# RWKV-7 and short-convolution block on one core: the off-diagonal 16x16 corners of the 32x32 inverses computed on VectorE instead of TensorE, and the last chunk's Gram blocks issued with the others

## The chip, the cores and the metric

The kernel runs on one core of one Trainium2 chip. The metric is the device time of one launch in microseconds; the time before is the median of three runs. Beside those, one execution was profiled.

## The reference, cut to what matters

A block takes 512 tokens of width 2048, prepends 16 meta tokens, normalises them and multiplies by one input projection of 65 column tiles of 128. Half of the columns feed a short gated convolution, the other half an RWKV-7 recurrence over 16 heads of 64. Both results go through an output projection, a residual and a last norm.

```
P = rmsnorm(h) @ w_in                      # r, k, v, g, lora | B, C, h, gc
S_t = S_{t-1} diag(w_t) - (S_{t-1} kk_t)(kk_t*a_t)^T + v_t k_t^T
y_t = S_t r_t
y_a = (groupnorm(y) + bonus) * silu(g);   y_b = B * conv3(C*h) * silu(gc)
out = rmsnorm(h + concat(y_a, y_b) @ w_out)[meta:]
```

The recurrence is run in nine chunks of 64 steps (the meta tokens are padded to the first). In chunk form every head and chunk needs the inverse of a 64x64 unit-like triangular matrix built from the Gram products of its keys. That inverse is what the change is about.

## The kernel before

The input projection is one long stream of matmuls, the generator `mains` (line 483). Its tiles follow `plan` (line 102): k, r and v of a pair of heads, g, and then C, h, B and gc of the convolution. One tile is 16 steps of three matmuls (high and low parts of weights and activations), for k, v, r, g, C and h in two column halves, so 96 matmuls and two PSUM banks; B and gc have 48 of 512 columns and one bank. The banks come from the pool `pm`, which has four. The tile's result is evacuated by `use` (line 400), mostly on VectorE (`scaled`, line 346). Weights are loaded by `prefetch` (line 138) into three raw buffers and split by `split_w` into six quarter slots: ScalarE casts the high part (line 134), VectorE or GpSimd subtracts the low part (line 135). The column offset of a quarter in its slot comes from `column` (line 115).

All else is placed in this stream by hand. TensorE's order is the program's order. `fill(ns)` (line 551) advances the stream by so many ns of projection, counted as 0.43 ns a column, and `later(ns, fn)` (line 532) traces a DMA when the clock of the stream has come so far; such DMAs are queued on SyncE behind the last weight load that was traced. The other engines' orders are chosen by a scheduler from priorities and expected times; `ahead()` raises a priority, and `issue_after` puts instructions behind a given one on its engine, without waiting for its result.

For each pair of heads i, `prepare(i)` (line 627) makes the operands, then the Gram blocks (`gram`, line 679): nine chunks and two heads, 18 matmuls of 64x128, eight chunks in one group and chunk 8 in a second group after `fill(FW["gram2"])`, together with the key norms `n2` and the bonus sums `zb`. `masked` (line 688) takes them to SBUF as `gt` on VectorE. The triangles go to DRAM (`sg`), and their 16x16 diagonal blocks come back as `d`, one block per partition, 72 partitions. VectorE inverts them there by doubling (lines 769 to 789) into `y`. The blocks of `y` go to DRAM into `sx` (`blocks`, line 737), from which `load_inverse` (line 793) reads 64x64 matrices `xT` and, at swapped partitions, `xo`.

After every two pairs, `invert` (line 831) joins the blocks in two levels on TensorE. Level one makes the 16x16 corners of the 32x32 inverses: transposes `xn` on VectorE (line 844), a group of 64 matmuls (line 853), a copy to SBUF on ScalarE (line 860), a second group of 64 (lines 867 and 869), and then on VectorE a copy under the mask `ms` (line 877), transposes `xm` (line 880) and a copy of half of it to `xo` (line 884). Level two does the same with 32x32 blocks (lines 893 to 918). The result is stored to DRAM for the recurrence (`recur`, line 940), which follows the last `invert` and is again woven into the stream. Then `split_mix` and the output projection finish the kernel.

Of the kernel before, what the change touches and what calls it, by code (L numbers as in the profile page):

```python
# [18 lines left out]
P = 128  # L19
# [5 lines left out]
CH = 64  # L25
# [16 lines left out]

FW = dict(
    evac=34, start=1062, lora=2200, gram=8000, gram_b=13500, gram2=5500, misc=2000, v=2000, vt=1000, solve=24500, solve_first=30000,
    tr=3200, lev=3000, cp=4200, out=1500, begin=19500, p=2900, u=2900, s=5200, last=3700, mix=2600,
)


# [29 lines left out]
def hymba_kernel(ctx: ExitStack, tc: tile.TileContext, xt, xtok, front, w_in, w_out, pv, lup, cst, msk, gf, out):  # L78
# [84 lines left out]
    ms = cq.tile([P, CH], I32, name="ms")  # L163
    ident = cs[:, C_ID : C_ID + P]
    gmask = cs[:, C_GM : C_GM + 256].rearrange("p (h c) -> p h c", h=2)
    pm = ph1.enter_context(tc.tile_pool(name="pm", bufs=4, space=PSUM))
# [119 lines left out]
        for kt in range(KT - 5, KT):  # L286
            square_x(kt)
    nc.sync.dma_start(cs, cst)
    nc.sync.dma_start(ms, msk)
    zt = tm("zt")  # L290
    nc.gpsimd.memset(zt, 0.0)
    for b in range(2):
# [43 lines left out]
    def main(j, ranges, name):  # L336
        prefetch(2 * j + 4)
        ps = banks(ranges, name, pm, "main")
        for k4 in range(4):
            if k4 == 1:  # L340
# [56 lines left out]
    def behind_of(what):  # L397
        return tc.issue_after(state.pop(what)) if what in state else nullcontext()

    def use(what, i, ps):  # L400
        if what == "lora":
            use_lora(ps)
        elif what in ("k", "v"):
            t = cq.tile([P, LP], F32, tag=what, name=f"{what}{i}")
            nc.gpsimd.memset(t[:, META:CH], 0.0)
            shift_full(ps, tile_of[what] + i, f"{what}{i}", padded(t))
            got[what, i] = t
        elif what in ("r", "g"):
            t = cq.tile([P, SEQ], F32, tag=f"r{i % 2}" if what == "r" else "g", name=f"{what}{i}")
            shift_real(ps, tile_of[what] + i, f"{what}{i}", t)  # L410
            if what == "g":
                gate(t, f"r{i}")
                later(14000, lambda: nc.sync.dma_start(gated[i], t))
            got[what, i] = t
        elif what == "C":
            u = tm(f"u{i}")
            scaled(TAIL, ps, u, 14)
            got[what, i] = u
        elif what == "h":
            u = got["C", i]  # L420
            hh = tm(f"hh{i}")
            with behind_of("turned"):
                scaled(TAIL, ps, hh, 14)
            n = SEQ + 2
            nc.gpsimd.tensor_tensor(out=u[:, 0:n], in0=u[:, 0:n], in1=hh[:, 0:n], op=ALU.mult)
            cv = tp.tile([P, SEQ], F32, tag="cw", name=f"cv{i}")
            nc.scalar.activation(cv, u[:, 0:SEQ], AF.Copy, scale=col(V_CW, i))
            for j in (1, 2):
                nc.vector.scalar_tensor_tensor(
                    out=cv, in0=u[:, j : j + SEQ], scalar=col(V_CW, 8 * j + i), in1=cv, op0=ALU.mult, op1=ALU.add  # L430
                )
            got[what, i] = cv
# [21 lines left out]
    ready = set()  # L454
    direct = {}

    def token_scale_sums():
# [74 lines left out]
    def later(ns, fn):  # L532
        pending.append((clock[0] + ns, fn))
        pending.sort(key=lambda e: e[0])
# [92 lines left out]
    def prepare(i):  # L627
# [82 lines left out]
        zn = pi.tile([2, 288], F32, tag="misc", name=f"n2_{i}")  # L710
        zs = ((zn, 0, 288), (ze[0][0:2, P : P + 288], 288, LP))
        for z, a, b in zs:
            nc.tensor.matmul(z, ones[:, P : P + 2], sqh[:, a:b], start=True, stop=False)
            nc.tensor.matmul(z, ones[:, P : P + 2], sql[:, a:b], start=False, stop=True)
# [3 lines left out]
        with ahead():  # L718
            for z, a, b in zs:
                nc.scalar.copy(n2[0:2, a:b], z)  # L720
            masked([z[:, 0:P].unsqueeze(1) for z in ze], 8, 9)
        nc.scalar.copy(r, zb)
        fill(FW["misc"])

# [76 lines left out]
                    ),  # L801
                )

        later((22500 if i == 1 else 20500) if p else 29000, lambda: nc.sync.dma_start(blocks(sx), y))
        later((24500 if i == 1 else 22500) if p else 33000, load_inverse)

        for h, hs, ho in heads:
            for b in range(2):
# [17 lines left out]
                    64 * (1 - b // 2) + 32 * t, 32,  # L826
                )
        fill(FW["vt"])
        return dict(gt=gt, xT=xT, xo=xo, i=i)

    def invert(two):
        first = two[0]["i"]
        both = range(2)
        fill(FW["solve"] + 2400 * (first == 2) if first else FW["solve_first"] + 1100)
        run_pending(float("inf"))


        def wide(name):
            return tr(name)[:, 0 : 8 * CH].rearrange("p (q k s) -> p q k s", q=2, s=CH)
# [2 lines left out]
        with ahead():  # L842
            for q in both:
                state["turned"] = nc.vector.transpose(
                    xn[q][:, CH:LP], two[q]["xT"][:, 1:NCH].rearrange("p c s -> p (c s)")
                ).ins
        fill(FW["tr"])
        z = [pz.tile([P, 2, 4, CH], F32, tag="tz", name=f"t{first}_{e}") for e in range(2)]
        for q in both:
            for k in range(4):  # L850
                for e, c in ((0, 2 * k + 2), (1, 2 * k + 1)):
                    for h, hs, ho in heads:
                        nc.tensor.matmul(
                            z[e][ho if e else hs, q, k], two[q]["gt"][hs, h, c, 0:CH],
                            xn[q][hs, c * CH : (c + 1) * CH], start=True, stop=True,
                        )
        ts_ = [wide(f"ts{first}_{e}") for e in range(2)]
        with ahead():
            for e in range(2):
                nc.scalar.copy(ts_[e], z[e])  # L860
        fill(FW["lev"])
        z = [pz.tile([P, 2, 4, CH], F32, tag="tz", name=f"z{first}_{e}") for e in range(2)]
        for q in both:
            xT, xo = two[q]["xT"], two[q]["xo"]
            for k in range(4):
                for h, hs, ho in heads:
                    nc.tensor.matmul(z[0][hs, q, k], ts_[0][hs, q, k], xT[hs, 2 * k + 2], start=True, stop=True)
                for h, hs, ho in heads:
# [3 lines left out]
        xn = [tr(f"xm{t['i']}") for t in two]  # L872
        with ahead():
            for q in both:
                xT, xo = two[q]["xT"], two[q]["xo"]
                for e in range(2):
                    nc.vector.copy_predicated(
                        xT[:, 2 - e : NCH : 2], ms.unsqueeze(1).to_broadcast([P, 4, CH]), z[e][:, q]
                    )
                nc.vector.transpose(xn[q][:, CH:LP], xT[:, 1:NCH].rearrange("p c s -> p (c s)"))  # L880
            for q in both:
                xT, xo = two[q]["xT"], two[q]["xo"]
                for h, lo, hi in quads:
                    nc.vector.tensor_copy(xo[other[h], :, 32:CH], xT[hi, 1 : NCH - 1 : 2, 32:CH])
        fill(FW["cp"])
# [641 lines left out]
```

## Time and profile before

| | us |
|---|---|
| median of 3 runs | 1006.29 (1004.66 to 1007.55) |
| profiled execution | 1006.95 |
| its span | 1005.2 |
| TensorE matmul busy | 993.7 (99%) |
| TensorE weight load busy | 913.6 (91%) |
| VectorE busy | 680.5 (68%) |
| ScalarE busy | 393.2 (39%) |
| GpSimd busy | 264.2 (26%) |

The time of an execution is its span plus 1.75 us that lie around it. Busy time is the union of an engine's instructions; matmuls overlap, so a matmul of 0.28 us can be followed by the next after 0.12. In the rows of a timeline the first number is the start within the span, the second the length, and x the number of instructions merged into the row.

### The profile page before, as it was taken

The page shows a single profiled execution, that of the slowest core. Times are in us where ns is not written, and L with a number is a line of the kernel's source. Part 1 is how long each engine was busy: PE and PEld are TensorE (multiplying, and loading weights), DVE is VectorE, ACT ScalarE, POOL GpSimd, SP SyncE. Part 2 cuts the span into 40 slices and gives each one's busy share as a digit, 9 for nine tenths or more (in the row PEclk, how much of TensorE's full clock was granted, in tenths as well). Part 3 has the DMA queues.
Part 4 walks back from the last instruction along what each step waited for, and adds up shares of the span by engine and source line. Part 5 has one row for each costly group of instructions (what it writes and reads, how often), then busy time and mean ns, then how long its engine had stood idle before and what let it go on. Part 6 is the DMA issues. An engine that isn't in the chain of part 4 may idle for free.

```text
span 1005.2 us, 23750 instructions
## 1 busy us (share of the span) xinstructions
PE 993.7 (99%) x9723; PEld 913.6 (91%) x9723; DVE 680.5 (68%) x1313; ACT 393.2 (39%) x729; POOL 264.2 (26%) x286
## 2 busy tenths in 40 slices
PE   9999999999999999999999999999999999999996
PEld 8999998999998999998999998989888898788886
DVE  6777965587775568655668654245554597899996
ACT  7553422344323434323434322223232435545553
POOL 0122323224222323232423222223332333001001
PEclk9999999999999999999999999999999999999998
DMA  9525476446674363864273855978673689688644
GB/s 329 151 83 146 124 191 152 146 119 152 144 185 148 103 169 91 224 159 119 85 171 98 222 143 167 341 243 249 202 226 91 174 270 238 197 267 236 151 105 168
DMA packets 185181, 175.35 MB, mean 174 GB/s; under 512 B 121584, under 2 KB 142832, under 8 KB 184560
## 3 DMA queue, kind: packets, MB, share of 16 engines
q1 hardware_dynamic: 182480, 164.92, 56.4%
q0 software_dynamic: 2304, 8.39, 5.0%
q8 instruction: 76, 1.25, 0.5%
q10 hardware_dynamic: 288, 0.52, 0.1%
q14 instruction: 33, 0.27, 0.1%
HBM read 137.44 MB, written 36.35 MB: 173 GB/s over the span
## 4 chain that ended last, share of the span: by engine, by line
PE 65%; DVE 3%; DMA 1%; ACT 1%; SPq 0%; issue 0%; DVEq 0%; POOL 0%; ACTq 0%
PE ps_gc L328 8%; PE ps_B L328 7%; PE ps_h L328 7%; PE ps_C L328 6%; PE M L1243 5%; PE ps_k L328 5%; PE ps_v L328 5%; PE ps_g L328 5%; PE ps_r L328 5%; PE P L1243 4%; PE Q L1243 2%; PE zy L1010 1%; PE zs L1006 1%; PE g L681 1%; PE rz L954 1%; DVE o L1216 1%
## 5 line engine op out<-in xcount | busy, mean ns | idle before, releaser
L135 POOL TENSOR_TENSOR w<-wr,w 128x512 fp32r<-128x512 f32 x119 | 166.6, 1401 | 366.8 <-ACT w L134 306.2
L134 ACT CAST w<-wr 128x512 fp32r<-128x512 f32 x252 | 153.0, 618 | 280.7 <-PE ps_C L328 46.2
L135 DVE TENSOR_TENSOR w<-wr,w 128x512 fp32r<-128x512 f32 x133 | 95.8, 727 | 102.3 <-ACT w L134 92.2
L328 PE MATMUL ps_k<-xh,w 128*128 128x256 f32 (+1 forms) x512 | 95.8, 285 | 0.1
L328 PE MATMUL ps_r<-xh,w 128*128 128x256 f32 (+1 forms) x512 | 95.1, 281 | 0.0
L328 PE MATMUL ps_v<-xh,w 128*128 128x272 f32 (+1 forms) x512 | 95.0, 283 | 0.0
L328 PE MATMUL ps_h<-xh,w 128*128 128x258 f32 (+1 forms) x512 | 94.1, 282 | 0.0
L328 PE MATMUL ps_C<-xh,w 128*128 128x258 f32 (+1 forms) x512 | 93.2, 281 | 0.0
L328 PE MATMUL ps_g<-xh,w 128*128 128x258 f32 (+1 forms) x512 | 91.9, 281 | 0.0
L328 PE MATMUL ps_B<-xh,w 128*128 128x512 f32 x256 | 83.4, 395 | 0.1
L328 PE MATMUL ps_gc<-xh,w 128*128 128x512 f32 x256 | 81.7, 393 | 0.3 <-DVE w L135 0.3
L328 PEld LDWEIGHTS ps_h<-xh,w 128*128 128x128 f32 x512 | 79.7, 189 | 1.8 <-issue 1.2
L328 PEld LDWEIGHTS ps_k<-xh,w 128*128 128x128 f32 x512 | 80.4, 189 | 0.7 <-DVE w L135 0.3
L328 PEld LDWEIGHTS ps_r<-xh,w 128*128 128x128 f32 x512 | 80.3, 189 | 0.2
L328 PEld LDWEIGHTS ps_v<-xh,w 128*128 128x128 f32 x512 | 80.0, 189 | 0.3
L328 PEld LDWEIGHTS ps_C<-xh,w 128*128 128x128 f32 x512 | 79.7, 189 | 0.6
L328 PEld LDWEIGHTS ps_g<-xh,w 128*128 128x128 f32 x512 | 79.3, 189 | 0.3
L328 PE MATMUL ps_k<-xl,w 128*128 128x272 f32 (+1 forms) x256 | 72.9, 285 | 0.0
L328 PE MATMUL ps_v<-xl,w 128*128 128x256 f32 (+1 forms) x256 | 72.5, 283 | 0.0
L328 PE MATMUL ps_r<-xl,w 128*128 128x256 f32 (+1 forms) x256 | 72.4, 283 | 0.0
L328 PE MATMUL ps_g<-xl,w 128*128 128x256 f32 (+1 forms) x256 | 72.3, 282 | 0.0
L328 PE MATMUL ps_C<-xl,w 128*128 128x256 f32 (+1 forms) x256 | 72.0, 281 | 0.0
(320 smaller groups left out, 2261.9 us busy)
## 6 DMA issues: line engine op xcount, KB each, us to landing
wr<-in_w_in_dram SPq DMA_DIRECT2D x126, 512.0 KB
ct<-opd SPq DMA_DIRECT2D x64, 288.0 KB
wo<-in_w_out_dram SPq DMA_DIRECT2D x21, 512.0 KB
x<-in_w_out_dram POOLq DMA_DIRECT2D x16, 512.0 KB, 5.8
opd<-ar SPq DMA_DIRECT2D x8, 576.0 KB
opd<-gt SPq DMA_DIRECT2D x16, 288.0 KB
opd<-bt SPq DMA_DIRECT2D x64, 64.0 KB
x<-in_w_out_dram SPq DMA_DIRECT2D x8, 512.0 KB
```

Of the source, the lines that this page charges most:

```text
L134: nc.scalar.copy(hi, rq)
L135: low[q] = eng.tensor_tensor(out=lo, in0=rq, in1=hi.bitcast(F32), op=ALU.subtract).ins
L328: nc.tensor.matmul(ps[r], ww[:, w], xx[:, kt, a:b], start=(kt == 0 and n == 0), stop=(kt == KT - 1 and n == 2))
L681: nc.tensor.matmul(z[h][:, c - c0], bk[hs, c, h : h + 2, :].rearrange("p a s -> p (a s)"), ar[hs, c].rearrange("p a s -> p (a s)"), start= ...
L954: nc.tensor.matmul(z[e][ho if e else hs, 0, k], t[hs, o : o + CH], t[hs, O_V : O_V + CH] if part else st[hs, 4 * e + k], start=(part == 0 ...
L1006: nc.tensor.matmul(d[hs, j], w, x[hs], start=(a == 0), stop=(a == b - 1))
L1010: nc.tensor.matmul(d[ho, j], t[hs, o : o + CH], x[hs], start=(a == 0), stop=(a == b - 1))
L1216: nc.vector.tensor_tensor(out=lo, in0=rq, in1=hi.bitcast(F32), op=ALU.subtract)
L1243: nc.tensor.matmul(bank[s], left(prod, jj, m, s), w, start=(jj == 0 and n == 0), stop=(jj == 7 and n == 2))
```

## The change

Level one leaves TensorE. `prepare` writes `y` to DRAM once more, as whole rows of 256 (`sy`). `invert` loads from `sg` the off-diagonal 16x16 blocks (`d12`) and from `sy` the inverted diagonal blocks (`y11`, `y22`), for two pairs of heads and two halves of each 16-row block on 2 x 2 x 32 = 128 partitions, 8 rows each. Six products on VectorE (a multiply of 512 elements and a reduction each) form `y11 * d12 * y22`, which `put_corners` writes into `sx`; only then `load_both` loads `xT` and `xo` of both pairs. The groups of lines 853, 867 and 869, their copies, the mask `ms` and its load go. The second level and its transposes stay.

With it: chunk 8's Gram blocks are issued in the group of the other eight, into two banks of `pm`, and masked with them; `n2` takes the bank that they had. Evacuations (`use`) traced after the products are queued behind the last reduction, and some weight subtractions and convolution taps behind the transposes `xn`. The weight slots of k, r and lora move to offset 80, k's two column halves run in natural order, the Gram group of pairs 0, 1 and 3 is moved by 2.0, 2.5 and -4.0 us of the stream, and three `sums` of the output stage come one or two units earlier. The fills in `invert` are longer: from the end of `prepare` to the second level 44.2 us of stream instead of 38.1 (48.8 instead of 44.7 in the first, 46.6 instead of 40.5 in the second).

```diff
-    tr=3200, lev=3000, cp=4200, out=1500, begin=19500, p=2900, ...
+    tr=3200, lev=3000, cp=4200, out=1500, begin=19500, pairs=16000, corner=25000, p=2900, ...
...
-        return {"B": 0, "gc": 0, "v": 80, "g": 80, "h": 80}.get(what, 16)
+        return {"B": 0, "gc": 0, "C": 16}.get(what, 80)
...
-            for r in (1, 0) if name[0] == "k" else range(len(ranges)):
+            for r in range(len(ranges)):
...
+    def use(*tile_):
+        with behind_of("corner"):
+            used(*tile_)
...
-        fill(FW["gram_b" if p else "gram"])
+        shift = {0: 2000, 1: 2500, 3: -4000}.get(i, 0)
+        fill(FW["gram_b" if p else "gram"] + shift)
...
-        for c in range(8):
-            gram(za if c < 4 else zc, c, c // 4 * 4)
+        ze = [pm.tile([P, 1, P], F32, tag="main", name=f"g{i}_8_{h}") for h in range(2)]
+        for c in range(NCH):
+            gram((za, zc, ze)[c // 4], c, c // 4 * 4)
         masked(za, 0, 4)
         masked(zc, 4, 8)
-        fill(FW["gram2"])
-        ze = [pz.tile([P, P + 288 * (1 - h)], F32, tag="tz", name=f"g{i}_8_{h}") for h in range(2)]
-        gram([z[:, 0:P].unsqueeze(1) for z in ze], 8, 8)
+        masked(ze, 8, 9)
+        fill(FW["gram2"] - shift)
...
-        later((22500 if i == 1 else 20500) if p else 29000, lambda: nc.sync.dma_start(blocks(sx), y))
-        later((24500 if i == 1 else 22500) if p else 33000, load_inverse)
+        def put_blocks():
+            nc.sync.dma_start(sy.rearrange("(p s) -> p s", s=256), y.rearrange("p s t -> p (s t)"))
+            nc.sync.dma_start(blocks(sx), y)
+
+        later(16500 if p else 29000, put_blocks)
...
     def invert(two):
-        fill(FW["solve"] + 2400 * (first == 2) if first else FW["solve_first"] + 1100)
+        late = 4600 if first == 0 else 2400 * (first == 2)
...
+        later(9000, load_corners)
+        later(15700, load_pairs)
+        fill(FW["pairs"])
...
+        def product(dst, ni, nj, a, b, nk, name):
+            w = tr(f"pq{first}{name}")[:, 0 : ni * nj * nk].rearrange("p (i j k) -> p i j k", i=ni, j=nj)
+            nc.vector.tensor_tensor(out=w, in0=a, in1=b, op=ALU.mult)
+            state["corner"] = nc.vector.tensor_reduce(out=dst, in_=w, op=ALU.add, axis=AX.X).ins
+
+        with ahead():
+            for n, (r0, rn, k0) in enumerate(((0, 2, 0), (2, 2, 0), (4, 4, 8))):
+                product(
+                    at3(mid, 16 * r0, [[16, rn], [1, 16]]), rn, 16,
+                    at3(y11, 32 * r0 + k0, [[32, rn], [0, 16], [1, 16 - k0]]),
+                    at3(d12, 16 * k0, [[0, rn], [1, 16], [16, 16 - k0]]), 16 - k0, f"a{n}",
+                )
+            for n, (r0, rn, j0, kn) in enumerate(((0, 8, 0, 8), (0, 4, 8, 16), (4, 4, 8, 16))):
+                product(
+                    at3(y12, 16 * r0 + j0, [[16, rn], [1, 8]]), rn, 8,
+                    at3(mid, 16 * r0, [[16, rn], [0, 8], [1, kn]]),
+                    at3(y22, j0, [[0, rn], [1, 8], [16, kn]]), kn, f"b{n}",
+                )
+        later(FW["corner"] + late - 4900, put_corners)
+        later(FW["corner"] + late - 2700, load_both)
+        fill(FW["corner"] + late)
         run_pending(float("inf"))
...
+        splits_behind(state["turned"])
...
-                        nc.tensor.matmul(
-                            z[e][ho if e else hs, q, k], two[q]["gt"][hs, h, c, 0:CH],
-                            xn[q][hs, c * CH : (c + 1) * CH], start=True, stop=True,
-                        )
...
-                    nc.tensor.matmul(z[0][hs, q, k], ts_[0][hs, q, k], xT[hs, 2 * k + 2], start=True, stop=True)
-                for h, hs, ho in heads:
-                    nc.tensor.matmul(z[1][hs, q, k], ts_[1][ho, q, k], xo[ho, k], start=True, stop=True)
...
-        at(6 + n, sums, 1, (n,))
+        at((5, 5, 7, 9)[n], sums, 1, (n,))
```

More of the change, by code (lines that the diff above doesn't have):

```diff
@@ L44 @@
     evac=34, start=1062, lora=2200, gram=8000, gram_b=13500, gram2=5500, misc=2000, v=2000, vt=1000, solve=24500, solve_first=30000,
-    tr=3200, lev=3000, cp=4200, out=1500, begin=19500, p=2900, u=2900, s=5200, last=3700, mix=2600,
+    tr=3200, lev=3000, cp=4200, out=1500, begin=19500, pairs=16000, corner=25000, p=2900, u=2900, s=5200, last=3700, mix=2600,
 )
@@ L398, in behind_of, with used @@
         return tc.issue_after(state.pop(what)) if what in state else nullcontext()
-    def use(what, i, ps):
+    def use(*tile_):
+        with behind_of("corner"):
+            used(*tile_)
+    def used(what, i, ps):
         if what == "lora":
@@ L454, in hymba_kernel @@
     ready = set()
+    tardy = []
     direct = {}
@@ L802, in load_inverse @@
                 )
[L804 to L805 removed]
+        sy = dp.tile([NB * 256], F32, tag="sy", name=f"sy{i}")
+        def put_blocks():
+            nc.sync.dma_start(sy.rearrange("(p s) -> p s", s=256), y.rearrange("p s t -> p (s t)"))
+            nc.sync.dma_start(blocks(sx), y)
+        later(16500 if p else 29000, put_blocks)
         for h, hs, ho in heads:
@@ L828, in prepare, with splits_behind @@
         fill(FW["vt"])
-        return dict(gt=gt, xT=xT, xo=xo, i=i)
+        return dict(gt=gt, xT=xT, xo=xo, i=i, sg=sg, sx=sx, sy=sy, load=load_inverse)
+    def splits_behind(ins):
+        for i in [i for q, i in low.items() if state["quarter"] <= q - 6] + [i for t, i in tardy if t > clock[0] - 15000]:
+            if i.engine == ins.engine:
+                tc.add_manual_dep(
+                    i, ins.name, mybir.DependencyInfo(mybir.DependencyClass.NoSync, mybir.DependencyReason.DATA),
+                    reason="issue_after",
+                )
     def invert(two):
@@ L833, in invert @@
         both = range(2)
-        fill(FW["solve"] + 2400 * (first == 2) if first else FW["solve_first"] + 1100)
+        late = 4600 if first == 0 else 2400 * (first == 2)
+        hold = [tr(f"hold{first}_{n}") for n in range(2)]
+        d12, y11 = hold[0][:, 0:256], hold[0][:, 256:512]
+        y22, mid, y12 = hold[1][:, 0:256], hold[1][:, 256:384], hold[1][:, 384:512]
+        spots = [(t, slice(64 * q, 64 * q + 64)) for q, t in enumerate(two)]
+        halves = [(t, half, slice(64 * q + 32 * half, 64 * q + 32 * half + 32)) for q, t in enumerate(two) for half in both]
@@ new lines, in corner, with load_corners, load_pairs @@
+        def corner(t, half, step, rows):
+            return bass.AP(
+                tensor=t.tensor, offset=t.offset + 8 * BLK + 16 + half * CH, ap=[[2 * BLK, 32], [step * CH, rows], [1, 16]]
+            )
+        def load_corners():
+            for t, half, ps in halves:
+                nc.sync.dma_start(d12[ps].rearrange("p (s t) -> p s t", t=16), corner(t["sg"], 0, 1, 16))
+        def load_pairs():
+            for t, ps in spots:
+                y = t["sy"]
+                for x, at_, step, n in ((y11, 0, 16, 240), (y22, 256, 0, 256)):
+                    nc.sync.dma_start(
+                        x[ps, 0:n],
+                        bass.AP(tensor=y.tensor, offset=y.offset + 8 * 256 + at_, ap=[[step, 2], [512, 32], [1, n]]),
+                    )
@@ new lines, in put_corners, with load_both, at3 @@
+        def put_corners():
+            for t, half, ps in halves:
+                nc.sync.dma_start(corner(t["sx"], half, 2, 8), y12[ps].rearrange("p (s t) -> p s t", t=16))
+        def load_both():
+            for t in two:
+                t["load"]()
+        later(9000, load_corners)
+        later(15700, load_pairs)
+        fill(FW["pairs"])
+        def at3(x, o, dims):
+            return bass.AP(tensor=x.tensor, offset=x.offset + o, ap=[list(x.ap[0])] + dims)
+        def product(dst, ni, nj, a, b, nk, name):
+            w = tr(f"pq{first}{name}")[:, 0 : ni * nj * nk].rearrange("p (i j k) -> p i j k", i=ni, j=nj)
+            nc.vector.tensor_tensor(out=w, in0=a, in1=b, op=ALU.mult)
+            state["corner"] = nc.vector.tensor_reduce(out=dst, in_=w, op=ALU.add, axis=AX.X).ins
```

43 lines of the change are left out of this document (7 added, 36 removed).

## The prediction

> **What bounds the kernel now.** I read the page first, then what TensorE waited for, then its timeline around the groups of small matmuls, and last the timelines of VectorE, ScalarE and the queue of SyncE between a Gram stage and the inverse that follows it. The page's first line and the waits of TensorE (engine, tile, line, who ended the wait: total us, times, longest):
>
> ```profile
> PE 993.7 (99%) x9723; PEld 913.6 (91%) x9723; DVE 680.5 (68%) x1313; ACT 393.2 (39%) x729; POOL 264.2 (26%) x286
> PE pwarm L187 <- DVE cold L184: 1.4, 1, 1.4
> PE zy L1010 <- issue: 0.9, 1, 0.9
> PE M L1243 <- DVE o L1216: 0.6, 2, 0.4
> ```
>
> TensorE is never without work for long: its waits, longest first, are three small ones and the rest below 0.6. So a matmul group that disappears is worth what the stream of matmuls spends on it, and a change elsewhere costs only where it makes TensorE wait. The big projection (line 328) is one stream of tiles of 96 matmuls, and all other groups are put between its matmuls, so removing a group pulls everything behind it forward.
>
> **The groups that go.** The level-16 step of each `invert` has two groups of 64 matmuls. The first invert, on TensorE (start, us, line, tile, count):
>
> ```profile
> 173.32 0.41 PE L328 MATMUL ps_k<-xh,w 128*128 128x272 f32 x2
> 173.66 1.16 PE L853 MATMUL t<-xn,gt 64*64 64x64 f32 x64
> 174.75 0.39 PE L328 MATMUL ps_k<-xl,w 128*128 128x272 f32 x1
> 174.98 0.40 PE L328 MATMUL ps_k<-xh,w 128*128 128x272 f32 x2
> ...
> 177.83 0.40 PE L328 MATMUL ps_k<-xh,w 128*128 128x272 f32 x2
> 179.25 0.39 PE L328 MATMUL ps_k<-xl,w 128*128 128x256 f32 x1
> 179.48 0.40 PE L328 MATMUL ps_k<-xh,w 128*128 128x256 f32 x2
> ```
>
> From 173.32 to 174.75 are 1.43 us, of which two projection matmuls would take 0.25 (174.98 to the next step goes at about 0.12 each): 1.18. The first projection matmul behind the group starts its successor after 0.23 instead of 0.12, so 0.11 more. One group costs 1.29, the second (177.83 to 179.25, then 0.23) 1.28. Four inverts of two groups: 8 x 1.29 = 10.3 us off the path. With them go two PSUM copies on ScalarE per invert and, on VectorE, four masked copies, two transposes and four partition copies; none of these was a wait of TensorE, so I count them at nothing.
>
> **The Gram blocks of chunk 8.** They are now issued with the other eight instead of in a group of their own:
>
> ```profile
> 79.54 2.06 PE L681 MATMUL g<-ar,bk 64*128 64x128 f32 x32
> 81.52 0.39 PE L328 MATMUL ps_r<-xl,w 128*128 128x256 f32 x1
> ...
> 87.38 0.28 PE L328 MATMUL ps_r<-xh,w 128*128 128x256 f32 x1
> 87.59 0.49 PE L681 MATMUL g<-ar,bk 64*128 64x128 f32 x4
> 88.01 0.29 PE L713 MATMUL n<-sq_h,ones 128*2 128x288 f32 x1
> 88.14 0.30 PE L714 MATMUL n<-sq_l,ones 128*2 128x288 f32 x1
> ```
>
> From 87.38 to 88.01 are 0.63, less 0.12 for the projection matmul: 0.51 goes. In the large group four matmuls more cost 4 x 1.98/32 = 0.25. Net 0.26, eight times: 2.1 us.
>
> **Weights at another offset, k in natural order.** k and v have the same shape; only the offset of the weight slot and the order of the two halves differ, and the change gives k what v has:
>
> ```profile
> 470.56 11.62 PE ps_k L328 x96
> 533.65 11.53 PE ps_v L328 x96
> ```
>
> 0.09 a tile, seven k tiles in that stream: 0.6 us; bounds 0 and 1. For r, which moves as well, I take nothing. The whole gain is 10.3 + 2.1 + 0.6 = 13.0 us.
>
> **What is added, on VectorE.** Six products, each a multiply of 512 elements with one operand at a stride of 16, and a reduction. The last step of the solve before is the same form:
>
> ```profile
> 398.45 2.06 PE L681 MATMUL g<-ar,bk 64*128 64x128 f32 x32
> 402.56 2.48 DVE L691 TENSOR_TENSOR gt<-g,cs 128x512 f32<-128x512 f32 x4
> 428.22 1.06 DVE L774 TENSOR_TENSOR prod<-d,y 72x512 f32<-72x512 f32 x1
> 429.31 0.68 DVE L780 TENSOR_REDUCE tt<-prod 72x64 f32<-72x512 f32 x1
> 431.49 0.68 DVE L789 TENSOR_REDUCE y<-prod 72x64 f32<-72x512 f32 x1
> 284.39 1.69 DVE L774 TENSOR_TENSOR prod<-d,y 72x512 f32<-72x512 f32 x1
> 283.87 1.29 POOL L135 TENSOR_TENSOR w<-wr,w 128x512 fp32r<-128x512 f32 x1 [4.35 <-ACT w L134]
> ```
>
> Multiply to reduction 1.09, reduction to an independent multiply 0.62 (2.48 for four): 1.71 x 6 = 10.3 us an invert. That it now fills 128 rows instead of 72 should not matter, rows run side by side. [...] The multiply at 284.39 took 1.69 beside the GpSimd operation in the last row: such company could add 0.6 to a product, 1.9 us if half of them meet it. [...]
>
> VectorE stands at 68%, so 10.3 us four times do not make it the bound. What counts is what queues behind: `use` now puts every PSUM evacuation traced after the products behind the last reduction. The rows that decide, third invert, from the chain, VectorE and SyncE:
>
> ```profile
> 421.83 11.25 PE ps_C L328 x96
> 408.14 0.29 DVE L691 TENSOR_TENSOR gt<-g,cs 128x128 f32<-128x128 f32 x1 [0.25 <-ACT n L720]
> 408.45 1.27 SPq L621 DMA_DIRECT2D sg<-gt  x2
> 415.94 0.17 DVE L764 TENSOR_TENSOR y<-tt,nd 72x8 f32<-72x8 f32 x1
> 420.43 0.42 DVE L352 TENSOR_TENSOR pr_g<-ps_g,rs 128x256 f32<-128x256 f32 x1 [4.32 <-PE ps_g L328]
> 432.20 0.30 SPq L804 DMA_DIRECT2D sx<-y  x1
> 434.75 0.60 SPq L795 DMA_DIRECT2D xT<-sx  x1
> 436.75 0.63 SPq L796 DMA_DIRECT2D xo<-sx  x1
> 439.19 0.71 DVE L844 STREAM_TRANSPOSE xn<-xT 128x512 f32<-128x512 f32 x1 [0.57 <-DMA xT<-sx]
> ```
>
> By the clock that the program keeps (0.43 ns a column), the products are traced 16 us behind the end of `prepare`, which falls some 2 us before C2 ends at 433.1. C2's evacuation then waits for the corner. C2 and h2 hold all four banks of `pm`, so B2, due 11.25 us after 433.1, at 444.3, needs C2's first bank: corner 10.3 plus one evacuation 0.42 plus its signal. The corner must start by 433.5, or TensorE waits for the difference. It starts when the diagonal blocks have gone to DRAM and back: from the end of y (the reduction at 431.49 ends at 432.2) to the first load 2.6 (432.20 to 434.75), three issues of 0.6, and 1.8 from the end of the last issue (437.4) to its user (439.19): 6.2 us. With y where it is now the corner starts at 438.4 and TensorE waits 4.9. But y comes sooner: sg is issued right behind the mask of chunk 8 (408.14 ends at 408.43), which in the merged group follows the four masks that end at 405.0, so some 2.8 earlier with its own 0.6; and the solve, ready at 416.1, stood 4.32 behind an evacuation that waited for TensorE, which an earlier start may pass. Between 0 and 4.9 I take 1.0 (y 4 us sooner), nearest to the 2.8 that the mask row shows plus a part of the 4.32. The same holds for the fourth invert (C3) and, with k2 behind h0 and gc0, for the first; the second, ahead of two one-bank tiles, has room. 3 x 1.0 = 3.0, bounds 0 and 14.7.
>
> The chunk-8 blocks now sit in two `pm` banks until masked, about 4.5 us after the group (group at 398.45 in pair 5, masks at 402.56 to 405.0). Where a Gram group ends less than that ahead of a tile's end (i = 3, and i = 4, which the longer fills move 1.3 us towards the end of v4) the next tile waits for a bank: 1.0 each, 2.0, bounds 0 and 4. The products' loads and stores (14 issues more an invert, 0.3 to 0.6 each) go on SyncE, which mostly waits for weight buffers and stays ahead; behind them stand the weight loads, covered by raw buffers a tile and a half ahead: 0, and if that cover were gone the price is in the slower rival. The second level now waits for eight loads after the corner; 2 x (436.75 + 0.63 - 434.75) + 1.8 = 7.1 us plus two transposes, against 25 us from products to transposes less corner and loads: 0, at most 1.6 an invert.
>
> **Sum.** The profiled execution took 1006.95 (span 1005.2), 0.66 above the median of 1006.29. 1006.95 - 13.0 + 3.0 + 2.0 = 998.95; against the median 998.3.
>
> **Rivals.** *No bank wait at all* (y 5 us sooner, or products as cheap as dense ones): 1006.3 - 13.0 = 993.3. For it speaks the 4.32 idle in front of the solve; against it that the chain has three DRAM trips. [...] *The waits eat the gain*: y stays late, 14.7 + 4 against 13.0, at or above 1006; by 3 us either way it is the same. *Slower, through ScalarE's order.* The convolution's scale stands in ScalarE's queue in front of weight casts:
>
> ```profile
> 157.93 0.72 ACT L427 ACTIVATE cv<-u,pvt 128x512 f32<-128x512 f32 x1 [12.74 <-POOL u L425]
> 158.56 2.17 ACT L134 CAST w<-wr 128x512 fp32r<-128x512 f32 x4
> 160.88 0.73 PE L328 MATMUL ps_gc<-xh,w 128*128 128x512 f32 x2 [0.27 <-DVE w L135]
> ```
>
> Four casts ran in a burst when the scale was done, and TensorE had just stopped: there is no slack. The scale waits for h0's evacuation, now behind the corner. If that is 14 us later (a corner of 10.3 and its loads) and the queue order stays, TensorE stands for about 14 us, and, taking half of it for h1, in front of whose end the products are traced too, 7 more: 1006.3 - 13.0 + 21 = 1014. It decides from the point where casts due within the corner stand behind the scale. Against it: the scheduler places instructions by when it expects them ready, and it knows of the corner.
>
> **Chances.** A change under 0.3% (3 us) can't be told from none here. Forecast (996 to 1003): 0.42. No wait (992 to 996): 0.29. Gain eaten, within 3 us of before: 0.10. ScalarE's order, or the bank waits at their worst: 0.19. So faster 0.71, same 0.10, slower 0.19. The range goes from 992 (no wait, with k's upper bound) to 1010, which takes in the waits at nearly their bounds and leaves out most of the slower rival.
>
> **What would show it.** Line 853's and 867's groups gone and line 681 with 36 matmuls in a group; TensorE's idle time up from some 3 us to 8, the new waits being projection tiles (B, k2, and tiles behind Gram groups) released by VectorE at line 352 or the masks; the corner's multiplies at 1.0 to 1.2 us. The forecast is wrong if TensorE's waits name weight splits (line 135) for many us, or if the products run in the middle of the tile with nobody waiting.

## The result, and the profile after

| | before | after |
|---|---|---|
| median, us | 1006.29 (5 runs, 1004.03 to 1007.65) | 1022.17 (5 runs, 1021.60 to 1023.12) |
| profiled execution / its span | 1006.95 / 1005.2 | 1021.6 / 1019.8 |
| mean granted clock of TensorE | 0.997 | 0.988 |

The change makes the kernel slower by 1.7%: ratio 1.0168, 95% interval 1.0156 to 1.018. The forecast was 998.3, range 992 to 1010. Line numbers move with the change: the projection is line 326, evacuations are line 351, the Gram masks line 697, the corner's products lines 895 and 896.

The page's busy line and clock row, and TensorE's waits (engine, tile, line, who ended the wait: total us, times, longest):

```profile
PE 987.6 (97%) x9211; PEld 911.5 (89%) x9211; DVE 708.6 (69%) x1321; ACT 390.7 (38%) x721; POOL 268.5 (26%) x286
PEclk9999998999999999989999989999999999999999
PE ps_B L326 <- DVE u L351: 9.2, 2, 4.6
PE ps_k L326 <- DVE hh L351: 5.6, 1, 5.6
PE ps_g L326 <- DVE gt L697: 1.8, 1, 1.8
PE ps_k L326 <- DVE gt L697: 1.3, 1, 1.3
PE g L687 <- DVE pr_v L351: 0.6, 1, 0.6
```

512 matmuls are gone, as they should be, but TensorE is busy only 6.1 us less, and it waits: all rows of this view add up to 24.1 us, against 3.4 before. 14.8 of them are three waits for a PSUM bank, released by evacuations of u and hh: B2, B3 and k2, the three tiles that the prediction named. And three of the clock's 40 slices show an 8 in the middle of the kernel, where before only the last slice did. The third inverse, on TensorE, VectorE and SyncE:

```profile
437.97 0.28 PE L326 MATMUL ps_h<-xh,w 128*128 128x256 f32 x1
...
449.11 0.28 PE L326 MATMUL ps_h<-xh,w 128*128 128x258 f32 x1
453.99 0.77 PE L326 MATMUL ps_B<-xh,w 128*128 128x512 f32 x1 [4.61 <-DVE u L351]
432.57 0.68 DVE L794 TENSOR_REDUCE y<-prod 72x64 f32<-72x512 f32 x1
...
442.17 2.04 DVE L895 TENSOR_TENSOR pq4a<-hold 128x512 f32<-128x512 f32 x2 [1.41 <-DMA hold<-sy]
...
453.44 0.81 DVE L351 TENSOR_TENSOR u<-ps_C,rs 128x256 f32<-128x256 f32 x3
433.28 0.31 SPq L812 DMA_DIRECT2D sy<-y  x1
...
434.05 1.25 SPq L622 DMA_DIRECT2D opd<-vs  x2
435.34 2.29 SPq L873 DMA_DIRECT2D hold<-sy  x4
```

The solve ends at 433.25. Its blocks go to DRAM, two stores of v stand ahead of the pair loads, and the first product starts at 442.17, after VectorE has stood idle for 1.41 us for the loads. C2 was complete at 438.0, but u's evacuation runs at 453.44, behind the last reduction. h2 ends at 449.4, B2 finds no bank and TensorE stands until 453.99. In the first inverse the way to the products is longer still:

```profile
148.06 0.68 DVE L794 TENSOR_REDUCE y<-prod 72x64 f32<-72x512 f32 x1
...
160.01 2.01 DVE L895 TENSOR_TENSOR pq0a<-hold 128x512 f32<-128x512 f32 x2 [7.73 <-DMA hold<-sy]
...
170.60 0.81 DVE L351 TENSOR_TENSOR hh<-ps_h,rs 128x256 f32<-128x256 f32 x3
152.58 2.34 SPq L873 DMA_DIRECT2D hold<-sy  x4
```

VectorE has nothing to do for 7.73 us, in which h0 is finished, and may not evacuate it.

The second loss shows only in windows laid right behind the three waits (busy us of PE, PEld, DVE, ACT, POOL, then granted clock, DMA share, GB/s), with one just ahead for comparison:

```profile
445.00:449.00 4.00, 4.00 (x37) 4.00 (x36) 3.93 (x5) 1.76 (x3) 1.29 (x1) 1.00 0.75 271
171.06:176.06 5.00, 5.00 (x24) 5.00 (x25) 3.67 (x7) 1.75 (x3) 2.90 (x2) 0.54 0.59 151
453.99:458.99 5.00, 5.00 (x12) 3.94 (x13) 1.59 (x6) 0.72 (x1) 1.29 (x1) 0.50 0.87 223
607.64:612.64 5.00, 5.00 (x12) 3.94 (x13) 1.58 (x6) 0.72 (x1) 1.28 (x1) 0.50 0.84 212
```

TensorE is busy all five microseconds and does half the work: 5 x (0.46 + 0.50 + 0.50) = 7.3 us. It counts as busy time, which is why busy time fell by 6 and not by 13.

### The profile page after: what moved, and what is told of

Same layout as the page of the kernel before. It is cut to its first block, busy times and chain, and to the rows that moved or that the text cites. A ratio compares the mean times of both kernels' runs of the same rounds, so it can differ in the third digit from the quotient of the medians.

```text
span 1019.8 us, 22856 instructions
## 1 busy us (share of the span) xinstructions
PE 987.6 (97%) x9211; PEld 911.5 (89%) x9211; DVE 708.6 (69%) x1321; ACT 390.7 (38%) x721; POOL 268.5 (26%) x286
## 4 chain that ended last, share of the span: by engine, by line
PE 72%; DVE 14%; DMA 5%; issue 3%; SPq 2%; POOL 2%; ACT 2%; DVEq 0%; POOLq 0%; ACTq 0%
PE ps_k L326 8%; PE M L1284 7%; PE ps_B L326 7%; PE ps_r L326 7%; PE ps_v L326 6%; PE ps_gc L326 6%; PE ps_g L326 5%; PE ps_C L326 5%; PE P L1284 4%; PE ps_h L326 4%; PE Q L1284 2%; DMA hold<-sy 2%; DVE w L135 1%; SPq L622 1%; PE ps_lora L326 1%
## 5 line engine op out<-in xcount | busy, mean ns | idle before, releaser
L135 POOL TENSOR_TENSOR w<-wr,w 128x512 fp32r<-128x512 f32 x119 | 171.6, 1443 | 342.8 <-ACT w L134 313.0
L326 PE MATMUL ps_k<-xh,w 128*128 128x256 f32 (+1 forms) x512 | 97.9, 288 | 6.9 <-DVE hh L351 5.6
L326 PE MATMUL ps_B<-xh,w 128*128 128x512 f32 x256 | 86.0, 407 | 9.2 <-DVE u L351 9.2
L326 PE MATMUL ps_k<-xl,w 128*128 128x256 f32 (+1 forms) x256 | 73.7, 288 | 0.0
L326 PE MATMUL ps_h<-xl,w 128*128 128x256 f32 (+1 forms) x256 | 72.3, 282 | 0.0
```

Of the source, the lines that this page charges most:

```text
L135: low[q] = eng.tensor_tensor(out=lo, in0=rq, in1=hi.bitcast(F32), op=ALU.subtract).ins
L326: nc.tensor.matmul(ps[r], ww[:, w], xx[:, kt, a:b], start=(kt == 0 and n == 0), stop=(kt == KT - 1 and n == 2))
```

## Experiments

Theory A: the three bank waits and the half clock behind them are the loss. Theory B: the products and their transfers slow the matmuls wherever they stand. Theory C: the merged Gram blocks cost it. Each ratio is against runs of the kernel before on the same chip.

**1. The products one tile later.**

```diff
-pairs=16000, corner=25000
+pairs=20000, corner=21000
```

> The changed kernel with the products traced 4 us later in the stream (and the rest of the inverse that much less behind them, so that the second level stays where it was). On VectorE one tile more is then evacuated ahead of the products in every inverse: h0 in the first, C2 and C3 in the third and fourth. Theory A (the three evacuations that stand behind the products starve TensorE of PSUM banks, 4.6 + 4.6 + 5.6 = 14.8 us, and the clock that the throttle then grants is half for some 4.7 us each, 2.35 x 3 = 7 us more): the waits at B2, B3 and k2 are gone and so are the three stretches at half clock; 1022.2 - 21.8 = 1000.4, plus up to 3 us in each of three inverses where TensorE now reaches the second level before its transposes: 1000 to 1009. Theory B (the products and their loads slow the matmuls themselves, wherever they stand): 1020 to 1024. Theory C (the merged Gram blocks cost it): 1020 to 1024.

Measured 1002.77 (ratio 0.9973, 0.9960 to 0.9986), and in a second session 1001.53 (0.9959, 0.9942 to 0.9975):

> The changed kernel with the products 4 us later, as measured before (1002.77, ratio 0.9973): the same again, ratio 0.995 to 0.999. If the earlier result was the chip's: 1.0 or above.

Four microseconds of the stream take 20 off the time. The third inverse now:

```profile
431.69 0.42 DVE L351 TENSOR_TENSOR u<-ps_C,rs 128x256 f32<-128x256 f32 x1 [0.43 <-PE ps_C L326]
...
435.57 2.04 DVE L895 TENSOR_TENSOR pq4a<-hold 128x512 f32<-128x512 f32 x2 [1.22 <-issue]
...
446.65 0.82 DVE L351 TENSOR_TENSOR hh<-ps_h,rs 128x256 f32<-128x256 f32 x3
442.62 0.28 PE L326 MATMUL ps_h<-xh,w 128*128 128x258 f32 x1
442.74 0.40 PE L326 MATMUL ps_B<-xh,w 128*128 128x512 f32 x1
```

u is out before the products, B2 follows h2 without a gap, and hh waits for the products without anyone missing its banks. The products themselves are the same, with the same 11 us and the same transfers, so B falls; C does too, since the merged Gram blocks are still there. This version beats both kernels; no version with all products was clearly better.

**2. No products, and four of six.**

```diff
-            for n, (r0, rn, k0) in ...: product(...)       # six products
+            state["corner"] = nc.vector.scalar_tensor_tensor(out=y12, in0=d12[:, 0:128], scalar=0.0, ...)
```

> The changed kernel with all six products left out (one VectorE operation that sets the corner blocks to zero takes their place, behind the same loads), so all loads, stores and waits for DMA stay and 10 us of VectorE work go. Theory A: with the operation at 160.0, 442.2 and 595.5 the evacuations behind it run before TensorE needs their banks: no bank wait, no slow stretch, 1022.2 - 21.8 = 1000.4, and the second level ready early. If the 14 more DMA issues of an inverse and their 14,400 packets were what costs: 1015 or more.

> The changed kernel with the last two of the six products of each inverse left out (a quarter of each corner block is set to zero instead, 0.2 us), so VectorE is done 2 x 1.71 - 0.2 = 3.2 us sooner. Theory A (bank waits, and a clock that falls to half only when TensorE has stood still for more than some 2 to 3 us): the waits fall from 4.6, 4.6 and 5.6 to 1.4, 1.4 and 2.4 us, the stretches at half clock go as well: 1022.2 - 9.6 - 7 = 1005.6. If the slow clock were in proportion to the wait, or had another cause: 1022.2 - 9.6 - 7 x 0.65 = 1008, or 1012.6.

Measured 1000.65 (0.9945, 0.9928 to 0.9961) and 1002.36 (0.9964, 0.9951 to 0.9978). With all loads and stores in place and only VectorE's time gone, the loss is gone, as A has it. With four products the bank waits were 1.8 at k2 and 0.7 for both B, and the clock behind the longest stayed whole:

```profile
PE ps_k L326 <- DVE hh L351: 1.8, 1, 1.8
PE ps_B L326 <- DVE u L351: 0.7, 2, 0.5
167.87:171.00 3.13, 3.13 (x26) 3.13 (x27) 2.14 (x5) 0.19 (x1) 1.29 (x1) 1.00 0.25 50
```

Two products fewer an inverse gave 19.8 us, more than the 16.6 expected: 14.8 - 2.5 = 12.3 of wait and the 7.3 of slow clock. The half clock isn't in proportion to the wait: 1.8 us cost none of it here. The limit of 2 to 3 us in the expectation was my estimate, and no run shows one: 1.84 us brought the half clock in experiment 4, and 3.24 us did not in experiment 5 (last section).

**3. TensorE kept busy while it waits.**

```diff
+        if name in ("B2", "B3"):
+            keep_busy(18)          # 128x512 matmuls into a bank of pz
...
+                if name == "k2" and k4 == 0 and r == 1:
+                    keep_busy(22)
```

> The changed kernel with matmuls that nobody reads (128x512, into a bank of pz) put on TensorE where it waits: 18 ahead of B2 and of B3 (18 x 0.23 = 4.1 us of the wait of 4.6) and 22 in k2 (5.1 of 5.6). They change no dependence. Theory A: the waits stay (the banks come free at the same time) but the projection behind them runs at full clock: the windows of 5 us behind the waits go from a granted clock of 0.50 to above 0.9, and the time falls by about 7 us to 1015. If the clock had nothing to do with the idle time (a throttle for power, theory B): 1022 or more, and the clock still drops.

```profile
452.37 0.47 PE L326 MATMUL ps_B<-xh,w 128*128 128x512 f32 x1 [1.08 <-DVE u L360]
452.37:457.37 5.00, 5.00 (x22) 4.17 (x23) 2.27 (x7) 1.23 (x2) 1.29 (x1) 1.00 0.84 220
171.71:176.71 5.00, 5.00 (x41) 5.00 (x42) 3.65 (x7) 2.01 (x4) 2.93 (x2) 1.00 0.59 157
PE zy L1060 <- issue: 5.4, 3, 3.0
```

The clock behind the waits is whole, with 22 matmuls in B2's first five microseconds instead of 12. The fourth gc tile starts at 614.7 instead of 621.0, so 6.3 of the expected 7 us are there. But the time was 1019.77 (1.0134, 1.0117 to 1.0151), only some 2.4 us less than after the change. The profiled run, the longest of the four, loses its lead again in the recurrence, which it began 5.9 us sooner (654.5 against 660.4) and whose last group of `zs` it reaches at the same time (782.1 and 782.3). The last row has three stops inside a group, put down to issue: 5.4 us, where the profile after has 1.2. Behind the longest (3.04, at 676.21) the clock was halved for 3.4 us, which costs 1.7. 4.2 + 1.7 are the 5.9. What TensorE stood for the profile doesn't show; that stays open. So at B2 the half clock came with the idle time (0.50 behind 4.6 us of it, 1.00 behind 1.08) and not with a load on the chip (DMA share 0.87 and 0.84), but its worth in time was not confirmed by this run alone.

**4. The parts alone.** The merge on the kernel before; the corner without the merge; the latter with the products 4 us later. The shifts of the Gram groups go with the merge.

```diff
-        ze = [pz.tile(...)]; gram(..., 8, 8) in a group behind fill(FW["gram2"])
+        ze = [pm.tile([P, 1, P], F32, tag="main", ...)]; all nine chunks in one group
```

> The kernel before with the merged Gram blocks of chunk 8 alone (in two banks of pm, with the shifts of the fills that go with them); the corner blocks stay on TensorE. Theory A: the merge saves 2.1 us of TensorE and its blocks make a tile wait for some 3 us: 1005 to 1008 against 1006.3. Theory C: above 1012. Theory B: as A.

> The changed kernel with the Gram blocks of chunk 8 back in a group of their own (in pz), without the shifts of the fills; the corner blocks stay on VectorE. Theory A: the bank waits of the corner stay at 13 to 16 us with their 7 us of slow clock, the 3.1 us of waits behind the merged Gram groups go, 2.1 us of group time come back: 1019 to 1023. Theory C (the merge is what costs, by the banks that it takes or by delaying the inverse): below 1010.

> The kernel without the merge and with the products 4 us later in the stream. Theory A: as the changed kernel with the products 4 us later (1002.8), less 2.0 us of waits behind the merged groups, plus 2.1 us of group time: 1001 to 1005. Theory C: 3 us or more below that kernel, under 1000.

The merge alone: 1004.60 (0.9984, 0.9972 to 0.9996), slightly faster. The corner alone: 1025.35 (1.019, 1.0171 to 1.021), beyond what I had expected and slower than the whole change by 2 us by the ratios, whose intervals overlap. With the products later: 1006.89 (1.001, 0.9998 to 1.0022), where 1001 to 1005 was expected. So C is wrong in the other direction: beside the corner the merge is worth some 2 to 5 us by the ratios. With it the inverse starts sooner: in the third one y ends 4.7 us ahead of C2's end, without it 3.3 (434.89 against 438.18). What the profile with the products later has over that of experiment 1 is two stretches at half clock, which cost 1.7 us each, behind a wait of 2.76 us for a weight split and one of 1.84 at the second level. With the corner alone and the products in their old place the bank waits grow:

```profile
PE ps_B L326 <- DVE u L351: 15.1, 2, 7.9
PE ps_k L326 <- DVE hh L351: 7.9, 1, 7.9
```

**5. A shorter way through DRAM.**

```diff
-        later(15700, load_pairs)
+        later(13700, load_pairs)
...
-                    14000 + 1000 * (2 * b + t), i, vs[...]
+                    14000 + 6000 * (i < 6) + 1000 * (2 * b + t), i, vs[...]
```

> The changed kernel with the pair loads of the corner put ahead of the stores of v on SyncE (2 us earlier in the stream, the stores 6 us later in the first six heads pairs): nothing but the way through DRAM from the end of the solve to the products is shortened. It measured 11.3, 9.0 and 9.2 us, where I had counted 6.2. Theory A: 1 to 2.5 us shorter each, the three waits shorter by the same and, where one falls to 2 us, without the half clock behind it: 1022.2 - 3 x (1 to 2.5) = 1014.7 to 1019, down to 1010 if the slow stretches go. If the loads' place in the queue doesn't matter: 1022.

Measured 1018.68 (1.0133, 1.0108 to 1.0159), in the expected range. In the profiled execution, the fastest of the four (1015.88), the first inverse's way falls from 11.3 to 8.7 us (148.73 + 0.68 to 158.07), and the waits by 1.4 to 2.1 us each:

```profile
148.73 0.68 DVE L794 TENSOR_REDUCE y<-prod 72x64 f32<-72x512 f32 x1
...
158.07 2.03 DVE L895 TENSOR_TENSOR pq0a<-hold 128x512 f32<-128x512 f32 x2 [5.61 <-DMA opd<-vs]
150.21 3.51 SPq L873 DMA_DIRECT2D hold<-sy  x4
PE ps_B L326 <- DVE u L351: 6.2, 2, 3.2
PE ps_k L326 <- DVE hh L351: 3.5, 1, 3.5
```

The loads' place in the queue is what was gained: their first issue comes 0.8 us behind y instead of 3.8, while the four issues take 3.5 us instead of 2.3. From the end of the last issue to the first product it is still 4.4 us (5.1 with the stores ahead), so the stores ahead are not what makes that last leg long. (The profile names a store of v as what ended the wait; the product reads only what the pair loads and the loads of `d12` bring.) In the third inverse the way shrinks only from 8.9 to 8.2 us; there y also ends 0.8 us sooner against C2's end.

**6. The order left to the scheduler.**

```diff
-        with behind_of("corner"):
+        with nullcontext():
             used(*tile_)
```

> The changed kernel with the evacuations no longer bound to come behind the products (use calls used directly). In VectorE's order u and hh then stand ahead of the products in the third and fourth inverse, hh, gc0 and the convolution in the first. Theory A: no bank wait and no stretch at half clock (21.8 us less), but the products now start only when h2 has ended, some 449 instead of 442, end near 461, and the blocks go through DRAM (12 us more) to transposes at 473 to 477, where TensorE now comes to the second level at 466: a new wait of up to 7 to 10 us in three inverses, with half clock behind it. 1010 to 1025, with the waits at the second level instead of at B and k. If the order bound by hand were merely a mistake: 1000.

Measured 1040.23 (1.0348, 1.0332 to 1.0364): worse than expected, and by another wait than I had named. u and hh do go first; the products then start at 461.12, when h2 is evacuated, and the next weight split stands at their end:

```profile
461.12 3.17 DVE L895 TENSOR_TENSOR pq4a<-hold 128x512 f32<-128x512 f32 x2
...
473.51 0.68 DVE L135 TENSOR_TENSOR w<-wr,w 128x512 fp32r<-128x512 f32 x1
PE ps_B L326 <- DVE w L135: 15.3, 2, 7.6
PE ps_k L326 <- DVE w L135: 8.6, 1, 8.6
```

A third such wait, of 6.8 us, stands at a gc tile. The products block VectorE for 11 to 14 us wherever they stand. What counts is what falls due in that time: here a weight split, after the change an evacuation. Binding the order by hand was right; the place was not.

**7. Attempts to better the version of experiment 1.** The second level 3 us later; the Gram groups of i = 2 to 5 moved away from tile ends; both that and earlier pair loads; earlier pair loads alone.

```diff
-pairs=20000, corner=21000
+pairs=20000, corner=24000                       # shift4_late
...
-        shift = {0: 2000, 1: 2500, 3: -4000}.get(i, 0)
+        shift = {0: 2000, 1: 2500, 2: 1500, 3: -5000, 4: -4000, 5: 1500}.get(i, 0)   # shift4_gram
```

> As the kernel with the products 4 us later, but with the second level 3 us later in the stream as well, so that its transposes are done when TensorE gets there. Theory A: 1000 to 1003, no wait of more than 1 us at the second level. Theories B and C: 1020 to 1024.

> The kernel with the products 4 us later (1002.8), and the merged Gram groups of four head pairs moved in the stream so that they don't stand at the end of a projection tile (i = 4: 4 us earlier, i = 3: 1 more, i = 2 and 5: 1.5 us later, behind the evacuation that they wait for). The waits behind and in front of Gram groups there were 1.31 + 0.71 + 0.66 + 0.63 = 3.3 us. If these are bank waits as I read them: 999.5 to 1001. If they follow the groups wherever they stand: 1002 to 1004.

> As the kernel before this one in the list (products 4 us later, Gram groups moved), with the pair loads ahead of the stores of v too. The products of the first inverse then start some 1.5 to 2 us sooner, and the wait for a weight split behind them (1.3 us) goes: 998 to 1000.

> The same with the pair loads 2 us earlier in the stream, the stores of v where they were. In the first inverse the products start about 1 us sooner and the wait for a weight split behind them (1.3 us) shrinks to 0 to 0.5; the inverses come sooner for the second level too: 1001 to 1002.5, ratio to before 0.996. If a wait at the second level comes up as in the kernel with the moved stores (8.6 us there), it was the order of the loads and not the moved stores that made it: 1006 or more.

The first three missed: 1006.23 (1.0004, 0.9989 to 1.0019), 1011.16 (1.0057, 1.0039 to 1.0074) and 1016.96 (1.0111, 1.0092 to 1.013). The fourth gave 1001.60 (0.9962, 0.9950 to 0.9974), no different from the version that it started from.

```profile
PE t L934 <- DVE xn L922: 3.7, 3, 1.9
PE ps_g L326 <- DVE gt L697: 3.5, 1, 3.5
PE t L934 <- DVE xn L922: 8.6, 5, 3.0
```

The first row is of the second level later: the scheduler put the transposes behind gc2's gate, so the later place bought nothing. The next is of the moved Gram groups: a projection tile still waits for a mask, and the earlier groups wait for their operands (2.5 us). The last row is of the third kernel, whose second level came before its loads had landed. The rows alone don't give the loss. In the profiles of the three, TensorE waits 1.9, 3.8 and 7.8 us longer than in that of experiment 1, and behind stops of 1.6 to 3.5 us it ran at half clock for 10.2, 6.8 and 17.1 us, where that one has none before the end of its work; this costs half as much, 5.1, 3.4 and 8.5. The spans are 6.0, 6.3 and 14.8 us longer.

**8. What was left of the forecast gain.** The products left out and the merge undone.

> The changed kernel without the six products (corner blocks set to zero) and with the Gram blocks of chunk 8 back in their own group. Some 1006 - 10.3 of the groups that are gone = 996, if the 3.2 us of waits around the merged Gram groups (1.3 + 0.7 + 0.7 + 0.6) are what keeps the kernel without products above 993.3, since the merge would then be worth less than it costs: under 999. If the merge is worth its 2.1 us and more (it lets the inverse start earlier, and a later inverse makes the second level wait): 1002 or more.

Measured 996.86 (0.9913, 0.9899 to 0.9927), 3.8 us below the kernel without products that keeps the merge. Without the products the merge costs; beside them it pays.

## Why the prediction was wrong

The forecast's own terms, set beside the profile after (spans: 1005.2 - 13.0 + 5.0 = 997.2 forecast, 1019.8 measured, 22.6 apart):

| term | forecast, us | measured, us | difference |
|---|---|---|---|
| TensorE work saved | -13.0 | -13.4 (993.7 to 987.6, less 7.3 at half clock) | -0.4 |
| bank waits behind the corner | 3.0 | 14.8 | +11.8 |
| half clock behind them | none | 7.3 | +7.3 |
| other waits, over those before | 2.0 | 5.9 (24.1 - 14.8 - 3.4) | +3.9 |

The first row leans on the third. The profiles with as many matmuls and no half clock before the end (experiments 1 and 2) have 981.3 to 981.9 us busy, so the work saved is between 11.8 and 13.4.

**Right.** The groups' worth, 10.3: without products and merge the time is 8.7 under before by the medians, and in the profile TensorE's busy time falls by 11.7 (993.7 to 982.0) and its waits grow by 1.6 (3.4 to 5.0). The mechanism of the waits and the three tiles that would wait. That y comes about 4 us sooner against the stream: it ended 0.9 ahead of C2's end before and 4.7 ahead after (433.25 against 438.0). The reason given for it, the merged group, is only a part: with the corner alone the lead is already 3.3. Where that part comes from no run separates. The multiplies' length:

```profile
L895 DVE TENSOR_TENSOR pq4a<-hold x3: 1043/1057/1070, 442.2 to 445.3; 128x512 f32<-128x512 f32 x3
L895 DVE TENSOR_TENSOR pq6b<-hold x3: 1054/1627/1807, 600.5 to 604.2; 128x512 f32<-128x512 f32 x3
```

(shortest, median, longest in ns.) 1.06 on 128 rows, as line 774 had it on 72 before, and up to 1.8 beside a GpSimd subtraction (at 603.83, for 1.26 us), as the row of 1.69 had it.

**The step that failed first** is "between 0 and 4.9 I take 1.0" for each bank wait; 4.6, 4.6 and 5.6 were measured. The credit for an earlier y was due, and was eaten twice. "6.2 us" from the solve to the products took 8.9 in the third inverse and 11.3 in the first. In the third, the first load is issued 2.1 us behind y, two stores of v included, where I had 2.6; the kernel has four pair loads and not three, 2.3 us where I had 1.8; and from the end of the last issue to the first product it is 4.5 us (437.63 to 442.17) where I had 1.8 from other loads. That last leg is the error; why these loads land so late the runs don't show. In the first inverse SyncE came to the loads late as well: 3.8, 2.3 and 5.1. And "corner 10.3" took 11.3 in the third (442.17 to 453.44), one weight split and GpSimd's company included. 1.0 + 2.7 + 1.0 = 4.7 is the wait of 4.6. Experiment 5 shortened the way and the waits followed. That 14.8 came out at my bound of 14.7 is luck: the bound has y as late as before, a way of 6.2 and a corner of 10.3, and the earlier y made up for the longer way and corner.

**The step that was missing** is the clock. I priced a wait of TensorE at its length. Half clock was put at nothing without a word, and was 7.3 us. Experiment 2 shows that these waits cost about half as much again (19.8 us where the waits alone give 12.3), experiment 3 that the clock stayed whole, at 1.00, where TensorE didn't stand idle. Behind the wait of 4.6 us the trace has 0.50, and stops of 1.6 to 3.0 us brought the half clock too (experiments 3, 4 and 7 and the last section). At each of the three waits the half clock lasted 6.83 us, of which some 2 us fall into the wait itself; half of the 4.7 to 5.0 us behind it, three times, are the 7.3.

**The other waits** were under-sized: 3.1 us behind the merged groups (1.8 and 1.3) where I had 2.0, and 1.2 in front of them (pr_v 0.6, pr_k 0.6), where the group waits for a bank itself, which I had not thought of. k's 96 matmuls take 11.58 against 11.62, so that term was 0.3 and not 0.6.

**The rivals.** Without a bank wait 993.3: measured 1000.65 with no products at all, since the merge's waits and others stay. Products as cheap as the dense multiplies of line 691 (median 0.68) it did not get: 1.06. ScalarE's order: no such wait after the change; TensorE did starve for weights in experiment 6, but behind VectorE's products and not behind the convolution's scale. The rival in which the waits eat the gain came nearest: 14.8 us against its 14.7 and, around the merged groups, 4.3 against its 4. But y was not late, as it had it, and it has no half clock, so it comes to 1012 (1006.3 - 13.0 + 18.7) and not to 1022.

## What to carry to other kernels

Before a long piece of work goes to an engine that is half idle, list what falls due on that engine while it runs (evacuations, weight splits) and place it in a gap of that list; here one tile's difference in the order was worth 20 us. Price a stop of TensorE with the half clock behind it. In these profiles that was nothing behind stops of up to 1.5 us, 1.7 us behind some of 1.6 to 3.3 us and nothing behind others, and 2.3 to 2.5 us behind those of 4.6 to 5.6. Take the way through DRAM from the queue as it will stand, stores ahead of the loads included, and give the loads a landing time measured on loads like them: here 4.4 to 5.1 us, where others took 1.8.

## What the hardware showed

In these profiles the stretches at half clock ahead of the end of the work last 3.41 us or a multiple of it. Behind the three waits after the change (4.6 to 5.6 us) each lasted 6.83 us, of which 1.8 to 2.2 fall into the wait itself. Behind shorter stops it lasted 3.41, half of that (twice 6.83, at groups of small matmuls with more than one stop); behind stops of 6.8 to 8.6 us (the corner alone, and experiment 6) 6.83 or 10.24. The third inverse after the change, and the second wait of experiment 5 (2.96 us):

```profile
452.19:459.01 6.82, 5.02 (x12) 3.99 (x13) 3.39 (x10) 0.72 (x1) 1.29 (x1) 0.50 0.64 164
453.34:456.75 3.41, 2.82 (x7) 2.27 (x8) 1.57 (x7) 0.45 (x1) 1.92 (x2) 0.50 0.31 34
```

Whether a stop brought the half clock doesn't follow from its length alone. 1.99 us ahead of the first M of the output stage did so in one kernel (earlier pair loads, experiment 7), 1.98 us at the same place did not in another (experiment 1). And the next B of experiment 5 stood for 3.24 us and went on at full clock:

```profile
841.17 7.09 PE L1284 MATMUL M<-w,m 128*128 128x512 f32 x23 [1.99 <-DVE gc L351]
842.43:845.84 3.41, 3.41 (x10) 2.65 (x9) 2.08 (x3) 1.44 (x3) 0.36 (x1) 0.50 0.98 237
839.81 2.51 PE L1284 MATMUL M<-w,m 128*128 128x512 f32 x10 [1.98 <-DVE gc L351]
839.81:844.81 5.00, 5.00 (x22) 4.18 (x23) 4.11 (x7) 3.44 (x6) 0.86 (x1) 1.00 0.99 204
605.17 0.47 PE L326 MATMUL ps_B<-xh,w 128*128 128x512 f32 x1 [3.24 <-DVE u L351]
605.17:610.17 5.00, 5.00 (x22) 4.17 (x23) 2.27 (x7) 1.23 (x2) 2.93 (x2) 1.00 0.55 122
```

In the profiles of this case no stop of up to 1.5 us halved the clock, every one from 3.45 us up did, and those between went both ways. What decides between them the profiles don't show. So a stop of 2 us cost 1.7 us of clock besides in one kernel here, nearly as much as itself, and nothing in another.
